# Joined streams in the split projections, and an earlier residual and first weights in the last layer, in a two-layer attention and state-space backbone

## The chip, the cores and the metric

One core of one Trainium2 chip. The metric is device time in microseconds (us) of one launch. Differences of 0.2% are about the smallest that a measurement of this kernel tells from none.

## What is computed

Two layers on two streams of 256 tokens with 1024 features: the latent stream x and the context stream ctx. Layer 0 mixes tokens by attention, layer 1 by a state-space scan; each mixer and each feed-forward part (1024 to 4096, squared relu, back to 1024) ends in a residual, a gate and a layer norm. Only the latent stream leaves the last layer.

```python
h_lat = layer_norm(ALPHA * h_lat + g_m_l * y_lat, ln_mix_g[i], ln_mix_b[i])
f_lat = squared_relu_mlp(modulate(h_lat, sh_f_l, sc_f_l), ff_w1[i], ff_w2[i])
h_lat = layer_norm(ALPHA * h_lat + g_f_l * f_lat, ln_ff_g[i], ln_ff_b[i])
```

In layer 0 the context stream takes the same three lines with its own modulation. All is float32.

## The kernel before, in words

**Products.** Activations lie features by tokens: eight tiles of 128 features, each 512 columns wide, columns 0 to 255 latent (stream 0) and 256 to 511 context (stream 1). Each weight and each activation is split into a high part (rounded to the format fp32r) and a low part, and a product is three matmuls: high by high, high by low, low by high. `gemm` (L83) runs eight k steps of these three for one output tile of 128 features, with the weights stationary and 256 or 512 columns of activations moving. In the last layer `down` (L278) turns this round: 128 tokens stationary, 512 weight columns moving.

**Weights.** `emit_w` (L46) loads two units with one transfer of 1 MB into one of two raw buffers, on the SyncE queue, and splits each: a cast to the high part on ScalarE (L61), a subtraction for the low part on VectorE (L62), in two halves. The pairs lie in a ring of four (`wsp`); `next_w` (L64) prepares the pair it returns and two ahead. A cast into the ring waits until TensorE has finished with the pair that lay there.

**Split order in layer 0.** `proj` (L346) multiplies the eight output tiles once for each stream, 256 columns at a time, with the context stream three tiles (`LAG`) behind the latent one, so that the latent layer norm can start while context tiles run. After tiles 3 and 7 of a stream, `colsum` (L212) adds the residual's columns up for the mean. It is used for the attention output (name ao) and for the last chunk (c = 3) of the feed-forward part down (name f0b); the first chunk up (name f0a, c = 0) in `ff` (L404) has the same lag, so that latent hidden tiles cover the context norm. All other tiles of layer 0 run 512 columns at once (`proj_joint`, L366). `ln` (L260) normalises a stream and splits it; its names are lm00 and lm01 after the attention, lf00 and lf01 after the feed-forward part, the last digit being the stream. `mods_sums` (L139) builds the modulation vectors of layer 1 on VectorE (tiles ma) from transfers into tiles wm; it is woven into `ff`, but runs ahead of its place where VectorE is free.

**Last layer.** The scan runs in four groups; while the last one (`ssd`, tiles y) runs, the output projection's first 12 of 16 k steps are woven in (`so`, L1059). Then (L1068 to L1083) the residual is transposed from features by tokens to tokens by features into Xt (L1079 to L1081, tiles xr), and for each tile of 128 tokens the last four k steps run for each half of 512 features, `add_half` (L290) adds the gated product and takes statistics, and `ln_mid` (L311) normalises, transposes (tiles ut) and splits into u4h and u4l. Then (L1087 to L1097) the first 512 hidden features of each token tile are multiplied (f1r), squared and turned by `hidden_rows` (L388), four pairs of weights being taken from the ring. The other hidden tiles are f1a, the products down f. The rows for the last norm (`row`, L272) are loaded at L1099, and the residual is scaled and shifted by them in chunk 1 (L1121).

**Order.** The program is written as one sequence; a scheduler of the framework then plans, from its own cost estimates, in which order each engine issues, by place in the program where several are ready. Attention (and some groups marked in the code) keep the written order. Each engine and each queue then runs strictly in its planned order.

Of the kernel before, what the change touches and what calls it, by code (L numbers as in the profile page):

```python
# [8 lines left out]
F32 = mybir.dt.float32  # L9
# [10 lines left out]
LAG = 3  # L20
# [19 lines left out]
class Net:  # L40
# [270 lines left out]
    def ln_mid(self, i, x, st, aff, uh, ul):  # L311
# [5 lines left out]
        for q in range(2):  # L317
# [4 lines left out]
            for m in range(4):  # L322
# [3 lines left out]
                nc.scalar.activation(uh[k][:, c], p, AF.Identity, bias=sh, scale=sc)  # L326
# [5 lines left out]
                nc.vector.tensor_sub(ul[k][:, c], t, uh[k][:, c].bitcast(F32))  # L332
# [13 lines left out]
    def proj(self, nm, ah, al, g, streams, lag, sums):  # L346
        nc = self.nc
        ws = {}
        for t in range(8 + lag):
            for s in streams[::-1]:  # L350
                m = t - (lag if s == 1 else 0)
                if not 0 <= m < 8:
                    continue
                if m not in ws:
                    ws[m] = self.next_w()
                ps = self.bank("mm", f"{nm}{s}{m}")[:, :256]
                self.gemm(ps, ws[m], ah, al, 256 * s, 256 * s + 256)
                x = self.X[s][:, m, :]
                nc.vector.scalar_tensor_tensor(x, ps, g[:, s, m:m + 1], x, op0=ALU.mult, op1=ALU.add)
# [4 lines left out]
                yield s, m  # L364

    def proj_joint(self, nm, ah, al, g):  # L366
        nc = self.nc
        for m in range(8):
            w = self.next_w()
            ps = self.bank("mm", f"{nm}{m}")  # L370
            self.gemm(ps, w, ah, al, 0, 512)
            for s in range(2):
                x = self.X[s][:, m, :]
                nc.vector.scalar_tensor_tensor(x, ps[:, 256 * s:256 * s + 256], g[:, s, m:m + 1], x,  # L374
                                               op0=ALU.mult, op1=ALU.add)
            yield m
# [11 lines left out]
    def hidden_rows(self, i, ps, fs):  # L388
# [4 lines left out]
        nc.vector.tensor_mul(r, r, r)  # L393
        pt = self.bank("aux", f"rt{i}")
# [9 lines left out]
    def ff(self, nm, uh, ul, g, streams, sums, mid=None):  # L404
        for c in range(4):
# [12 lines left out]

            if c == 0:
                for t in range(8 + LAG):  # L420
                    if t >= LAG:
                        hid(t - LAG, [1])
                    if t < 8:
                        hid(t, [0])
                    yield
            else:
                for m in range(8):
                    hid(m, streams)
                    yield
            fh = [fs[m][1] for m in range(8)]  # L430
            fl = [fs[m][2] for m in range(8)]
            if c < 3:
                for m in self.proj_joint(f"{nm}b{c}", fh, fl, g):
                    yield
            else:
                for s, m in self.proj(f"{nm}b{c}", fh, fl, g, streams, LAG, sums if c == 3 else None):
                    if c == 3 and m == 7 and mid is not None:
                        mid(s)
                    yield
# [275 lines left out]
    def layer0(self):  # L715
# [39 lines left out]
        with tc.tile_pool(name="wm", bufs=2) as self.wm:  # L755
# [8 lines left out]
            with tc.tile_pool(name="t2", bufs=4) as self.t2:  # L764
# [4 lines left out]
                for s, m in self.proj("ao", oh, ol, mT[:, :, 16:24], (0, 1), LAG, sums):  # L769
# [115 lines left out]
    def ssm_in(self, g, uh, ul):  # L885
# [19 lines left out]
        xw = [sp.tile([128, 2, 512], F32, tag=f"xw{d}", name=f"xw{g}{d}") for d in range(2)]  # L905
# [125 lines left out]
    def layer1(self):  # L1031
# [11 lines left out]
        nc.scalar.activation(self.aneg, self.vec("alog"), AF.Exp)  # L1043
        with tc.tile_pool(name="dq", bufs=1, space=DRAM) as dqp:
            dq = dqp.tile([2, 64, 256], F32, name="dq")
            self.dq = dq
            with tc.tile_pool(name="sp", bufs=2) as sp:
                self.sp = _Multi(tc, sp, dict(cy=2, ct=1, B=1, C=2, xt0=2, xt1=2, xw0=1, xw1=1, Bt=1, xc=1,
# [9 lines left out]

                def so():  # L1059
# [7 lines left out]
        with tc.tile_pool(name="tk", bufs=1) as self.tk, tc.tile_pool(name="fp1", bufs=2) as fp:  # L1067
            X = self.tk.tile([128, 2, 1024], F32, name="Xt")  # L1068
            ws = [self.next_w(whole=True, ahead=0) for _ in range(4)]
            bn = [self.stat_tile(f"bm{i}") for i in range(2)]  # L1070
            for i in range(2):
                for h in range(2):
                    for k in range(12, 16):
                        self.down(acc, st(yh, k), st(yl, k), ws[k - 12], k, k == 15, (i,), (h,))
                    if h == 0:
                        for q in range(2):
                            pt = self.bank("aux", f"xr{i}{q}")
                            for m in range(4):
                                nc.tensor.transpose(pt[:, 128 * m:128 * m + 128],  # L1079
                                                    self.X[0][:, 4 * q + m, 128 * i:128 * i + 128], self.ident)  # L1080
                            nc.scalar.copy(X[:, i, 512 * q:512 * q + 512], pt)  # L1081
                    self.add_half(acc, i, h, self.gates[2], X[:, i, :], bn[i])
# [146 lines left out]
```

## Time and profile before

| what | value |
|---|---|
| median of 3 runs | 1158.67 us (1158.28 to 1159.89) |
| profiled execution, its time | 1158.66 us |
| profiled execution, span of its instructions | 1156.9 us |
| TensorE matmuls, busy | 1098.6 us, 95% of the span, 6976 instructions |
| weight loads of TensorE, busy | 905.6 us, 78% |
| VectorE busy | 836.0 us, 72% |
| ScalarE busy | 603.3 us, 52% |
| GpSimd busy | 47.4 us, 4% |
| read from memory | 180.41 MB, 157 GB/s over the span |

PE is TensorE, PEld its weight loads, DVE VectorE, ACT ScalarE, SP SyncE. Matmuls overlap in the records, since one starts before the one ahead has left the engine, so the time that one costs is read from start to start. The granted clock is a share of full speed; 1.00 is 2.4 GHz and 0.50 is 1.2 GHz.

### The profile page before, as it was taken

Reading aid. Unit: us, or ns where it says so; the run is one execution under the profiler, and the core shown is the slowest. Engines: PE = TensorE matmul, PEld = TensorE weight load, DVE = VectorE, ACT = ScalarE, POOL = GpSimd, SP = SyncE. Lnnn points to the kernel's source line nnn. Section 1 sums busy time; section 2 is a strip of 40 time slices with the busy share of each in tenths; the row PEclk is TensorE's granted clock in tenths of the full one; section 3 lists DMA queues with packets and bytes.
Section 4 is the critical chain, followed back from the end, with each engine's and each line's share of the span. In section 5 each row is a group of like instructions: output and inputs, shape, how many; then the busy total and the mean of one; then the engine's idle time right before and its main releaser. Section 6 shows DMA issues by size and latency. Waiting matters only on the chain.

```text
span 1156.9 us, 18520 instructions
## 1 busy us (share of the span) xinstructions
PE 1098.6 (95%) x6976; PEld 905.6 (78%) x6976; DVE 836.0 (72%) x1701; ACT 603.3 (52%) x1382; POOL 47.4 (4%) x79
## 2 busy tenths in 40 slices
PE   5989999998999999999999998999999996999996
PEld 4776776988988887878899876777777675898895
DVE  4499885769938667773434899989799778565566
ACT  4386776135412322421423747787879756454451
POOL 1200000004000000000000410000000000000000
PEclk9999999999999999999999999999999998999999
DMA  8833442532635466663223135444445653555552
GB/s 318 330 128 115 124 131 90 182 111 74 201 127 184 164 221 232 231 205 108 74 74 110 46 114 155 156 146 145 147 139 189 224 199 142 172 182 193 182 182 73
DMA packets 41433, 182.79 MB, mean 158 GB/s; under 512 B 4608, under 2 KB 5248, under 8 KB 28288
## 3 DMA queue, kind: packets, MB, share of 16 engines
q1 hardware_dynamic: 41056, 181.36, 46.5%
q8 instruction: 55, 0.90, 0.3%
q10 hardware_dynamic: 288, 0.26, 0.1%
q14 instruction: 34, 0.28, 0.1%
HBM read 180.41 MB, written 1.18 MB: 157 GB/s over the span
## 4 chain that ended last, share of the span: by engine, by line
PE 80%; DVE 9%; DMA 5%; ACT 4%; issue 1%; DVEq 0%; SPq 0%; ACTq 0%
PE f0a L87 5%; PE f0a L88 5%; PE f0b L87 5%; PE f0a L89 5%; PE f0b L88 5%; PE f0b L89 5%; PE y L998 3%; PE f L288 2%; PE f L287 2%; PE f L286 2%; PE f1a L89 2%; PE f1a L87 2%; PE f1a L88 2%; DMA wm<-in_w_mod 2%; PE q L78 2%; PE pt L79 2%
## 5 line engine op out<-in xcount | busy, mean ns | idle before, releaser
L61 ACT CAST wh<-raw 128x512 fp32r<-128x512 f32 x404 | 238.6, 621 | 368.1 <-PE f0b L88 127.4
L62 DVE TENSOR_TENSOR wl<-raw,wh 128x512 fp32r<-128x512 f32 x404 | 269.0, 688 | 109.8 <-ACT wh L61 109.1
L87 PE MATMUL f0b<-f0fh,wh 128*128 128x512 f32 (+1 forms) x320 | 113.6, 355 | 0.0
L87 PE MATMUL f0a<-u1h,wh 128*128 128x512 f32 (+1 forms) x320 | 111.4, 352 | 1.5 <-ACT u1h L193 1.5
L88 PE MATMUL f0b<-f0fl,wh 128*128 128x512 f32 (+1 forms) x320 | 111.6, 349 | 0.1
L88 PE MATMUL f0a<-u1l,wh 128*128 128x512 f32 (+1 forms) x320 | 111.5, 350 | 0.0
L89 PE MATMUL f0b<-f0fh,wl 128*128 128x512 f32 (+1 forms) x320 | 111.2, 348 | 0.0
L89 PE MATMUL f0a<-u1h,wl 128*128 128x512 f32 (+1 forms) x320 | 111.2, 349 | 0.0
L150 DVE SCALAR_TENSOR_TENSOR ma<-wm,cs,ma 128x1024 f32<-128x1024 f32 x70 | 89.0, 1283 | 23.9 <-DMA wm<-in_w_mod 23.8
L87 PEld LDWEIGHTS f0a<-u1h,wh 128*128 128x128 f32 x320 | 60.9, 192 | 10.7 <-ACT u1h L193 2.1
L87 PEld LDWEIGHTS f0b<-f0fh,wh 128*128 128x128 f32 x320 | 60.1, 188 | 10.5 <-issue 2.6
L88 PEld LDWEIGHTS f0b<-f0fl,wh 128*128 128x128 f32 x320 | 60.1, 188 | 9.9 <-issue 1.4
L88 PEld LDWEIGHTS f0a<-u1l,wh 128*128 128x128 f32 x320 | 61.1, 192 | 8.2 <-DVE ut L195 0.4
L89 PEld LDWEIGHTS f0a<-u1h,wl 128*128 128x128 f32 x320 | 61.1, 191 | 7.6
L89 PEld LDWEIGHTS f0b<-f0fh,wl 128*128 128x128 f32 x320 | 60.2, 188 | 8.3
L87 PE MATMUL f1a<-u4h,wh 128*128 128x256 f32 x224 | 63.5, 284 | 0.0
L89 PE MATMUL f1a<-u4h,wl 128*128 128x256 f32 x224 | 63.5, 283 | 0.0
L88 PE MATMUL f1a<-u4l,wh 128*128 128x256 f32 x224 | 63.5, 283 | 0.0
L981 ACT ACTIVATE W<-A,sT 128x128 f32<-128x128 f32 (+1 forms) x128 | 50.0, 458 | 5.7 <-PE y L998 5.1
L374 DVE SCALAR_TENSOR_TENSOR X<-f0b,mT,X 128x256 f32<-128x256 f32 x48 | 21.0, 479 | 43.9 <-PE f0b L89 43.9
L89 PE MATMUL x<-u2h,wl 128*128 128x512 f32 x128 | 51.3, 402 | 1.1 <-DVE wl L62 1.1
L88 PE MATMUL x<-u2l,wh 128*128 128x512 f32 x128 | 51.6, 403 | 0.0
(435 smaller groups left out, 2702.7 us busy)
## 6 DMA issues: line engine op xcount, KB each, us to landing
raw<-in_wall SPq DMA_DIRECT2D x102, 1024.0 KB, 5.0
wm<-in_w_mod SPq DMA_DIRECT2D x96, 512.0 KB, 4.5
A<-dq SPq DMA_DIRECT2D x32, 256.0 KB, 3.6
E<-dq SPq DMA_DIRECT2D x32, 256.0 KB, 3.4
X<-in_xT SPq DMA_DIRECT2D x8, 256.0 KB, 7.4
gate<-in_rows SPq DMA_DIRECT2D x2, 512.0 KB, 12.3
out_dram<-Xt SPq DMA_DIRECT2D x4, 256.0 KB, 2.0
mixg<-in_rows SPq DMA_DIRECT2D x1, 512.0 KB, 6.2
```

Source lines behind the costliest of these rows:

```text
L61: nc.scalar.copy(h, src[:, c])
L62: nc.vector.tensor_sub(l, src[:, c], h.bitcast(F32))
L78: self.mm = lambda *a, **k: self.tc.keep_in_program_order(self.nc.tensor.matmul(*a, **k))
L79: self.tr = lambda *a, **k: self.tc.keep_in_program_order(self.nc.tensor.transpose(*a, **k))
L87: mm(ps, wh[:, k, :], ah[k][:, c0:c1], start=(k == 0), stop=False)
L88: mm(ps, wh[:, k, :], al[k][:, c0:c1], start=False, stop=False)
L89: mm(ps, wl[:, k, :], ah[k][:, c0:c1], start=False, stop=(k == 7))
L150: nc.vector.scalar_tensor_tensor(t, wm, c, t, op0=ALU.mult, op1=ALU.add)
L286: mm(ps, lh(i), wh[:, c], start=(k == 0), stop=False)
L287: mm(ps, ll(i), wh[:, c], start=False, stop=False)
L981: nc.scalar.activation(W[:, h, o:o + l1 - l0], A[:, h, l0:l1], AF.Relu, scale=-1.0, bias=self.sT[:, st, r + h:r + h + 1])
L998: ins = mm(ps[64 * a:64 * a + 64, l0:l1], lh[:, hc:hc + 64], mv, start=(n == 0), stop=(n == 5))
```

## The change

`proj` and `proj_joint` become one function: without split, eight joint tiles; with split, four joint tiles, then tiles 4 to 7 of the latent stream, then those of the context stream. In `ff` the first chunk up runs four latent tiles, the same four for the context, then four joint ones. `LAG` is 4 instead of 3. In the last layer, the residual's transposes go into the woven loop `so`, into tiles that the scan has left (their pool now outlives the scan); the first three weight pairs of the hidden part go into tiles of their own (those in which the rows for the last norm will lie), and the fourth pair is prepared behind tile 0's last split; tile 0's first hidden rows are multiplied ahead of tile 1's norm; the squared rows are turned after hidden tiles 4 and 5; the rows for the last norm are loaded in chunk 1.

```diff
-LAG = 3
+LAG = 4
...
-        t = self.tk.tile([128, 1024], F32, tag="row", name=nm, bufs=4)
+        t = self.tk.tile([128, 1024], F32, tag="row", name=nm, bufs=6)
...
+    def res_rows(self, x, i, q):
+        nc = self.nc
+        pt = self.bank("aux", f"xr{i}{q}")
+        for m in range(4):
+            nc.tensor.transpose(pt[:, 128 * m:128 * m + 128], self.X[0][:, 4 * q + m, 128 * i:128 * i + 128], self.ident)
+        nc.scalar.copy(x[:, 512 * q:512 * q + 512], pt)
...
-    def proj(self, nm, ah, al, g, streams, lag, sums):
+    def proj(self, nm, ah, al, g, split=False, sums=None):
+        cut = 8 - LAG if split else 8
...
+        for m, ss in [(m, (0, 1)) for m in range(cut)] + [(m, (s,)) for s in range(2) for m in range(cut, 8)]:
+            if m not in ws:
+                ws[m] = self.next_w()
+            n = 256 * len(ss)
+            ps = self.bank("mm", f"{nm}{ss[0]}{m}")[:, :n]
+            self.gemm(ps, ws[m], ah, al, 256 * ss[0], 256 * ss[0] + n)
+            for i, s in enumerate(ss):
                 x = self.X[s][:, m, :]
-                nc.vector.scalar_tensor_tensor(x, ps, g[:, s, m:m + 1], x, op0=ALU.mult, op1=ALU.add)
+                nc.vector.scalar_tensor_tensor(x, ps[:, 256 * i:256 * i + 256], g[:, s, m:m + 1], x,
+                                               op0=ALU.mult, op1=ALU.add)
                 if sums is not None and m % 4 == 3:
...
+            order = [(m, streams) for m in range(8)]
             if c == 0:
-                for t in range(8 + LAG):
-                    if t >= LAG:
-                        hid(t - LAG, [1])
-                    if t < 8:
-                        hid(t, [0])
-                    yield
...
+                order = [(m, (s,)) for s in streams for m in range(LAG)] + order[LAG:]
+            for m, ss in order:
+                hid(m, ss)
+                yield
...
                     for k in range(12):
                         self.down(acc, st(yh, k), st(yl, k), self.next_w(whole=True), k, False)
+                        if k % 2 and k > 3:
+                            i, q = divmod((k - 5) // 2, 2)
+                            if q == 0:
+                                X.append(self.xwp.tile([128, 1024], F32, tag=f"xw{i}", name=f"Xt{i}"))
+                            self.res_rows(X[i], i, q)
                         yield
...
+            first_w = []
+            for n in range(3):
+                wh, wl = (self.tk.tile([128, 1024], F32R, tag="row", name=f"f1w{n}{p}", bufs=6) for p in "hl")
+                self.emit_w(self.wpos, [(wh[:, 512 * q:512 * q + 512], wl[:, 512 * q:512 * q + 512]) for q in range(2)])
...
+            def f1_rows(i):
+                ps = self.bank("aux", f"f1r{i}")
...
+                return self.rows_sq(i, ps)
...
             for i in range(2):
                 for h in range(2):
                     for k in range(12, 16):
                         self.down(acc, st(yh, k), st(yl, k), ws[k - 12], k, k == 15, (i,), (h,))
...
+                    self.add_half(acc, i, h, self.gates[2], X[i], bn[i])
+                if i:
+                    with tc.issue_after(turned[0].ins), tc.issue_after(turned[1].ins):
+                        first_w.append(self.next_w(whole=True, ahead=0))
+                    rows.append(f1_rows(0))
+                turned = self.ln_mid(i, X[i], bn[i], aff, u4h, u4l)
+            rows.append(f1_rows(1))
...
+                    if c == 0 and m < 6:
+                        self.rows_turn(m - 4, rows[m - 4], first)
...
                 if c == 1:
+                    ag, ab = self.row(2, "mixg1"), self.row(3, "mixb1")
+                    fg, fb = self.row(4, "ffg1"), self.row(5, "ffb1")
```

`ln_mid` now returns its last ScalarE and its last VectorE instruction of the splits (`turned`), and `hidden_rows` is cut in two: `rows_sq` (relu and square) and `rows_turn` (transposes and splits).

## Rows read from the trace of the kernel before

**Rows 1.** The chain of waits over the span, shares by engine (page part 4).

```profile
PE 80%; DVE 9%; DMA 5%; ACT 4%; issue 1%; DVEq 0%; SPq 0%; ACTq 0%
```

**Rows 2.** Stretches: length, busy us (instructions) by engine, granted clock, DMA share, GB/s.

```profile
237.80:241.10 3.30, 3.30 (x18) 3.30 (x17) 0.20 (x1) 0.00 (x0) 0.00 (x0) 0.50 0.89 333
275.40:278.60 3.20, 3.15 (x15) 3.15 (x15) 3.20 (x9) 1.47 (x3) 2.81 (x4) 0.50 0.02 5
279.00:315.00 36.00, 36.00 (x301) 35.95 (x300) 35.42 (x64) 19.00 (x44) 4.97 (x5) 1.00 0.51 162
...
953.00:960.30 7.30, 0.03 (x1) 0.00 (x0) 7.24 (x20) 5.81 (x15) 0.00 (x0) 0.84 0.41 145
...
991.00:1142.00 151.00, 151.00 (x935) 136.27 (x935) 87.43 (x159) 74.61 (x156) 0.00 (x0) 1.00 0.51 175
```

**Rows 3.** Waits of TensorE, 204 to 320 and 930 to 992: us, times, longest.

```profile
PE aosum L208 <- DVE X L359: 2.0, 2, 1.8
PE f0a L87 <- ACT u1h L193: 1.5, 1, 1.5
PE lm01wb L241 <- DVE lm01wd L240: 1.2, 1, 1.2
PE lm01wt L232 <- ACT lm01ws L229: 0.5, 1, 0.5
...
PE ut L321 <- DVE Xt L315: 7.3, 1, 7.3
PE rt L396 <- DVE rr L393: 3.2, 2, 1.8
```

**Rows 4.** Instructions by tile: count, ns (minimum/median/maximum), first and last start; f0a, f0b.

```profile
L89 PE MATMUL f0a<-u1h,wl x78: 281/283/284, 284.8 to 312.7; 128*128 128x256 f32 x78
...
L89 PE MATMUL f0b<-f0fh,wl x30: 279/279/280, 590.7 to 601.0; 128*128 128x256 f32 x30
...
L89 PE MATMUL f0b<-f0fh,wl x28: 397/398/398, 315.8 to 334.7; 128*128 128x512 f32 x28
...
L87 PE MATMUL f0a<-u1h,wh x25: 389/389/390, 569.6 to 585.9; 128*128 128x512 f32 x25
...
L87 PEld LDWEIGHTS f0a<-u1h,wh x320: 186/188/333, 257.6 to 585.7; 128*128 128x128 f32 x160
```

**Rows 5.** Timeline of VectorE in the output projection: start, us, instruction [idle time before].

```profile
230.74 1.28 DVE L150 SCALAR_TENSOR_TENSOR ma<-wm,cs,ma 128x1024 f32<-128x1024 f32 x1 [1.96 <-DMA wm<-in_w_mod]
...
263.65 0.47 DVE L359 SCALAR_TENSOR_TENSOR X<-ao,mT,X 128x256 f32<-128x256 f32 x1
```

**Rows 6.** Timeline of ScalarE before the latent norm; in brackets the idle time before.

```profile
241.43 1.14 ACT L61 CAST wh<-raw 128x512 fp32r<-128x512 f32 x2 [8.75 <-PE ao L88]
245.74 0.37 ACT L220 COPY lm00ms<-aosum 128x256 f32<-128x256 f32 x1 [3.17 <-PE aosum L208]
```

**Rows 7.** Timeline of TensorE in the last layer, between projection and hidden tiles.

```profile
941.67 1.04 PE L1079 MATMUL xr<-con,X 128*128 128x128 f32 x8
...
949.92 1.06 PE L321 MATMUL ut<-con,Xt 128*128 128x128 f32 x8
...
960.36 1.94 PE L321 MATMUL ut<-con,Xt 128*128 128x128 f32 x8 [7.33 <-DVE Xt L315]
961.95 0.77 PE L1094 MATMUL f1r<-wh,u4h 128*128 128x512 f32 x1
...
978.75 0.37 PE L87 MATMUL f1a<-u4h,wh 128*128 128x256 f32 x1
```

**Rows 8.** Groups of VectorE instructions, 942 to 960 and 960 to 970: busy us, mean ns.

```profile
L62 DVE TENSOR_TENSOR wl<-raw,wh 128x512 fp32r<-128x512 f32 x6 | 3.9, 675 | 0.0
...
L1121 DVE TENSOR_TENSOR Xt<-Xt,mixg 128x512 f32<-128x512 f32 x4 | 2.7, 685 | 0.0
```

**Rows 9.** DMA issues by line: KB each, us from issue to landing.

```profile
ffb<-in_rows SPq DMA_DIRECT2D x1, 512.0 KB, 8.6
```

**Rows 10.** Instructions on tiles ma, 279 to 315: count, ns, first and last start.

```profile
L150 DVE SCALAR_TENSOR_TENSOR ma<-wm,cs,ma x12: 1272/1277/1496, 283.0 to 312.4; 128x1024 f32<-128x1024 f32 x12
```

More of the change, by code (lines that the diff above doesn't have):

```diff
@@ L331, in ln_mid @@
                     nc.vector.tensor_scalar(t, p, sc, sh, op0=ALU.mult, op1=ALU.add)
-                nc.vector.tensor_sub(ul[k][:, c], t, uh[k][:, c].bitcast(F32))
+                v = nc.vector.tensor_sub(ul[k][:, c], t, uh[k][:, c].bitcast(F32))
+        return a, v
     def ln_out(self, i, x, st, g, b):
@@ L363, in proj @@
                     self.colsum(sums[s], [(n, self.X[s][:, n, :]) for n in range(m - 3, m + 1)])
[L364 to L376, printed above, removed]
+            yield ss[-1], m
     def hidden(self, ps, c0, c1, fh, fl):
@@ L393, in hidden_rows, with rows_turn @@
         nc.vector.tensor_mul(r, r, r)
+        return r
+    def rows_turn(self, i, r, fs):
+        nc = self.nc
         pt = self.bank("aux", f"rt{i}")
@@ L417, in hid @@
                 self.hidden(ps, c0, c1, fh, fl)
+            order = [(m, streams) for m in range(8)]
             if c == 0:
-                for t in range(8 + LAG):
-                    if t >= LAG:
-                        hid(t - LAG, [1])
-                    if t < 8:
-                        hid(t, [0])
-                    yield
[L426 to L429, printed above, removed]
+                order = [(m, (s,)) for s in streams for m in range(LAG)] + order[LAG:]
+            for m, ss in order:
+                hid(m, ss)
+                yield
             fh = [fs[m][1] for m in range(8)]
             fl = [fs[m][2] for m in range(8)]
[L432 to L439, printed above, removed]
+            for s, m in self.proj(f"{nm}b{c}", fh, fl, g, c == 3, sums if c == 3 else None):
+                if c == 3 and m == 7 and mid is not None:
+                    mid(s)
+                yield
     def rope(self, dst, src):
@@ L768, in layer0 @@
                 nc.scalar.activation(warm[:, 0:1], self.eps, AF.Sqrt)
-                for s, m in self.proj("ao", oh, ol, mT[:, :, 16:24], (0, 1), LAG, sums):
+                for s, m in self.proj("ao", oh, ol, mT[:, :, 16:24], True, sums):
                     if m == 7:
@@ L904, in ssm_in @@
         G["xt"] = [sp.tile([128, 2, 512], F32, tag=f"xt{d}", name=f"xt{g}{d}") for d in range(2)]
-        xw = [sp.tile([128, 2, 512], F32, tag=f"xw{d}", name=f"xw{g}{d}") for d in range(2)]
+        xw = [self.xwp.tile([128, 2, 512], F32, tag=f"xw{d}", name=f"xw{g}{d}") for d in range(2)]
         Bt = sp.tile([128, 2, 128], F32, tag="Bt", name=f"Bt{g}")
@@ L1043, in layer1 @@
         nc.scalar.activation(self.aneg, self.vec("alog"), AF.Exp)
+        self.xwp = self.ctx.enter_context(tc.tile_pool(name="xwp", bufs=1))
         with tc.tile_pool(name="dq", bufs=1, space=DRAM) as dqp:
@@ L1057, in layer1 @@
                 st = lambda y, k: (lambda i: y[k % 8][:, 256 * (k // 8) + 128 * i:256 * (k // 8) + 128 * i + 128])
+                X = []
                 def so():
@@ L1067, in layer1 @@
         with tc.tile_pool(name="tk", bufs=1) as self.tk, tc.tile_pool(name="fp1", bufs=2) as fp:
-            X = self.tk.tile([128, 2, 1024], F32, name="Xt")
             ws = [self.next_w(whole=True, ahead=0) for _ in range(4)]
+            first_w = []
+            for n in range(3):
+                wh, wl = (self.tk.tile([128, 1024], F32R, tag="row", name=f"f1w{n}{p}", bufs=6) for p in "hl")
+                self.emit_w(self.wpos, [(wh[:, 512 * q:512 * q + 512], wl[:, 512 * q:512 * q + 512]) for q in range(2)])
+                self.wpos += 1
+                self.wout += 1
+                first_w.append((wh, wl))
+            self.fp = _Multi(tc, fp, dict(fh=9, fl=9, r=2, q=2))
+            pair = lambda m: tuple(self.fp.tile([128, 256], F32R, tag=t, name=f"f1{t}{m}") for t in ("fh", "fl"))
+            first = [pair(m) for m in range(4)]
+            def f1_rows(i):
+                ps = self.bank("aux", f"f1r{i}")
+                c = slice(128 * i, 128 * i + 128)
+                for k in range(8):
+                    wh, wl = (w[:, 512 * (k % 2):512 * (k % 2) + 512] for w in first_w[k // 2])
+                    nc.tensor.matmul(ps, u4h[k][:, c], wh, start=(k == 0), stop=False)
+                    nc.tensor.matmul(ps, u4l[k][:, c], wh, start=False, stop=False)
+                    nc.tensor.matmul(ps, u4h[k][:, c], wl, start=False, stop=(k == 7))
+                return self.rows_sq(i, ps)
             bn = [self.stat_tile(f"bm{i}") for i in range(2)]
+            rows = []
             for i in range(2):
@@ L1127, in layer1 @@
                         self.down(acc, lh(m), ll(m), ws[m - 4], 24 + m, m == 7, (i,), (h,))
[L1128 to L1129 removed]
+                    self.add_half(acc, i, h, self.gates[5], X[i], bn[i])
+                self.ln_out(i, X[i], bn[i], fg, fb)
     def chain(self, *gs):
```

43 lines of the change are left out of this document (4 added, 39 removed).

## The prediction

> **What bounds the kernel now.** I read the chain of waits first, because it says which engine's work the end hangs on: TensorE carries 80% of it [rows 1]. So only two things shorten the run: fewer TensorE microseconds, or fewer gaps in them. The table by stretches shows where the gaps are [rows 2]: in 279 to 315 us TensorE is busy for all 36 us, in 953.0 to 960.3 for 0.03 of 7.3. The waits of TensorE name them [rows 3]. In layer 0 it waits 2.0 us for column sums of the attention output, then 0.5, 1.2 and 1.5 us in the layer norm of the context stream; in the last layer 7.3 us for the normalised rows of the second token tile and 3.2 us for the squared rows. Two of the gaps are paid twice: after them the granted clock is 0.50, the lower of its two levels, 237.8 to 241.1 and 275.4 to 278.6 [rows 2].
>
> **A. Joined tiles.** Four of eight output tiles at each of three places (attention output, first feed-forward chunk up, last chunk down) become one 512-column product instead of two of 256. One tile is 8 x 3 products, so 96 pairs a place. Start to start, from first and last start over count [rows 4]: 256 columns take (312.7 - 284.8)/(3 x 77) = 0.1208 us where the modulation sums still run, 0.1184 in the last chunk; 512 columns take (334.7 - 315.8)/(3 x 27) = 0.2333 just after the first, (585.9 - 569.6)/(3 x 24) = 0.2264 before the second. Two places give 96 x (0.2416 - 0.2333) = 0.8 each, the third 96 x (0.2368 - 0.2264) = 1.0: **2.6 us**. Ends: 1.9 with 0.2333 at the third place too, 3.9 with 0.2264 everywhere; I keep each place with the stretch it is nearest to. VectorE still adds each stream by itself, so nothing is saved there.
>
> Joining also halves the weight loads of those tiles. One shows 0.188 us [rows 4], but a product starts every 0.1208, so the loads run beside the products, and I count nothing for them.
> The Trainium skill, TensorE: Matmul & The Clock Gate, Part 3 under "The mechanism", says that a weight load overlaps a product in flight only when the row groups differ; these loads and products all use the full 128 rows. By that rule the 288 loads saved would add 288 x 0.188 = 54 us. The trace does not agree with it.
>
> A joined first tile needs the context columns of the last head pair, which the half tile did not, but only in the last of its eight k steps, and seven (21 x 0.2333 = 4.9 us) stand before that. I count 0; without that cover it is at most the half tile that now runs beside the end of attention, 24 x 0.1208 = 2.9.
>
> **B. Context norm.** The order becomes joint 0 to 3, latent 4 to 7, context 4 to 7, then latent hidden 0 to 3 before context hidden. The norm of the context stream is now covered by four latent hidden tiles instead of three: 24 x 0.1208 = 2.9 us against the 3.2 us that TensorE waits there. Its start does not come later: the last context add stood on VectorE until 263.65 [rows 5], behind the splits of the latent stream, and these start from the last latent tile as before. With the gap nearly gone I also give back the half clock: 3.2 us hold 15 products that take 1.8 at 0.1208, so 1.4. **4.3 us**; ends 0 (VectorE decides, below) and 4.6.
>
> **C. Column sums.** 1.8 of the 2.0 us is one wait at 236.6. VectorE was late because a modulation sum ahead of the add had waited 1.96 us for its transfer [rows 5]; half clock follows, 1.4 again. Now the sums come behind joint tile 3, with four latent tiles that need none of it. But the modulation sums stay on the same queue, and whether one is late depends on a transfer. Ends 0 and 3.2; no row is nearer to either, I take the middle, **1.6 us**.
>
> Weights in the split tiles: four prepared pairs are live there, and the next cast on ScalarE waits until a context tile has let go of its pair, as it does now (idle 8.75 us before the cast at 241.43 [rows 6]). The pairs for tiles 4 to 7 become free while joint tiles of 5.6 us run, so TensorE does not see it. Cost 0; the loss if it is queued badly is a rival.
>
> **D. Last layer.** Reference is 941.67, where the first quarter of the last products ends, to 978.75, where the hidden tiles start: 37.1 us [rows 7].
> - Products: 36 x 0.2264 = 8.2. The transposes of tile 0 now are ready under them: second half at 2.7, then the 4.5 us of add, statistics and normalising that the trace shows (941.67 + 1.0 of residual transposes + 2.7 = 945.4, to 949.92), so 7.2. Transposes 1.1, up to 0.5 for the first split: 9.8.
> - First hidden rows of tile 0, 24 x 0.2264 = 5.4, now run while tile 1 is added and normalised. The fourth weight pair is cast only after tile 0's last split (queued on ScalarE and VectorE), and k steps 6 and 7 are behind it on TensorE, and tile 1's transposes behind those: a cast and a subtraction of 0.6 to 0.7 us each, some 1.2 us late. 16.4.
> - Tile 1: from transposes to first product 961.95 - 960.36 = 1.6; rows 5.4: 23.4. Both waits for squared rows fall, since hidden tiles 4 and 5 run meanwhile; the turns themselves stay, 1.3: 24.7.
> - The residual's 16 transposes (1.04 for eight) are paid in the y group instead: 2.1. Each also takes one of three auxiliary banks and a ScalarE copy there; the next y sums wait for them at most a copy's 0.6.
> - The first three pairs have places of their own, so their six subtractions on VectorE come before the normalising of tile 0 and no longer after the products. I charge three of six, 3 x 0.6 = 1.8 (six took 3.9 [rows 8]), since they are due before the adds in program order.
> 37.1 - 24.7 - 2.1 - 1.8 = **8.5 us**. Helping: VectorE spends 2.7 us on four instructions with one row for the last norm in the critical stretch [rows 8], and as much on four with the other. These eight and their two scalings on ScalarE now come in chunk 1, at no cost: VectorE is busy 87 of 151 us there, ScalarE 75 [rows 2]; without that cover it is their 5.4 us. Ends: 3.1 if tile 0's rows do not cover tile 1 (8.5 - 5.4), 10.3 if the subtractions cost nothing.
>
> The four row transfers leave the y group for the hidden stage. There the DMA engines are 0.51 busy (991 to 1142 [rows 2]); I count 0. If they all go ahead of a weight load, it lands as late as the fourth row did, 8.6 us after issue [rows 9], against 5.6 us for two pairs: 3 us.
>
> **Sum.** 2.6 + 4.3 + 1.6 + 8.5 = 17.0. The profiled execution took 1158.66 (span 1156.9), the median of the runs is 1158.67, so no correction: **1141.7 us**. All low ends give 5.0 us, all high ends 22.0.
>
> **Rivals.**
> 1. VectorE decides in layer 0. For: it is busy 35.42 of 36 us in 279 to 315 [rows 2]. Against: twelve of its instructions there, 1.28 us each, are modulation sums [rows 10] that nothing waits for yet. Then A's first two places, B and C come to nothing: 1.0 + 8.5 = 9.5, 1149.2 us.
> 2. The order planned for the last layer runs tile 1's work ahead of tile 0's rows, or the fourth pair comes so late that they cover nothing. For: the late fourth pair. D loses 5.4: 1147.1 us.
> 3. Slower. ScalarE runs in order. In the two places where a norm follows, the casts of the four next pairs wait for the four context tiles, and if they stand ahead of the copy of the latent sums, the latent norm starts up to 4 x 24 x 0.1208 = 11.6 us late instead of 0.7. Price 10.9 + 1.4 of clock, twice, 24.6: 1158.7 - 17.0 + 24.6 = 1166.3 us. It decides from the third cast: 8.0 + 1.4, twice, is 18.8. For: a cast that waited 8.75 us stood directly ahead of the copy at 245.74 [rows 6]. Against: that cast was done 3 us before the copy could run.
> 4. The change moves its waits and removes none: the context norm comes as much later as its cover grows, and tile 1's rows come as late as now because the first pairs' subtractions push them back. For: VectorE is shared by all of these. Against: they are 3.6 us, not 17. Then only A counts, half of it given back: 1157.4 us.
> 5. Weight loads stand in the way of products and joining removes them: 17.0 - 2.6 + 54 = 68, 1090 us. Against: 0.1208 is less than one load.
> The Trainium skill page named above is the source of this one; its rule is what the 0.1208 us speak against.
>
> **How the numbers follow.** Forecast 0.55, rivals 0.17, 0.16, 0.07, 0.04 and 0.01. A measurement of this kernel tells about 0.2% (2.3 us) from no change. Faster: 0.55 + 0.17 + 0.16 + 0.01 = 0.89; same 0.04; slower 0.07. The range runs from 1135 (just beyond the high ends) to 1152 (rival 1, with the 3 us of the row transfers): it holds the forecast with rivals 1 and 2, 0.88, less a little for their tails.
>
> **What would show it.** Right: 512-column products at 0.227 to 0.233 us for four tiles at three places; no wait of TensorE above 1 us around the context norm and no granted clock of 0.5 there; the 7.3 us wait replaced by one of 1 to 2 us; no wait for squared rows. Wrong: hidden tiles at more than 0.121 us a product (rival 1); a wait of several us ahead of tile 0's rows, or of their sixth k step (rival 2); a cast that idles ScalarE ahead of the copy of the sums (rival 3); the y group more than 2 us longer (rival 4).

## The result, and the profile after

| | before | after |
|---|---|---|
| median (lowest to highest), us | 1158.47 (1156.68 to 1159.89) | 1147.36 (1145.92 to 1150.04) |
| ratio, 95% interval | | 0.9915 (0.9898 to 0.9932) |
| profiled execution: time, span, us | 1158.66, 1156.9 | 1150.04, 1148.2 |
| TensorE matmuls, busy us, instructions | 1098.6, 6976 | 1095.5, 6688 |
| VectorE, ScalarE busy, us | 836.0, 603.3 | 834.3, 600.1 |

The change makes the kernel 11.1 us faster by the medians, 9.8 by the ratio (0.0085 x 1158.47), where 17.0 was forecast. The profiled execution of after is 2.7 us above its median.

The shares of the chain of waits, the answer to [rows 1]: TensorE's fell from 80% to 75%, so waits for others weigh more than before.

```profile
PE 75%; DVE 10%; DMA 8%; ACT 5%; issue 2%; DVEq 0%; SPq 0%; ACTq 0%
```

TensorE's waits of after (us, times, longest), in the stretches of [rows 3] and, first, in 640 to 720 us, where the scan stage begins:

```profile
PE B L87 <- DVE z L875: 3.4, 1, 3.4
PE x L87 <- DVE cy L800: 1.6, 1, 1.6
...
PE aosum L208 <- DVE X L368: 2.7, 2, 1.5
PE f0a L87 <- ACT u1h L193: 0.3, 1, 0.3
...
PE ut L329 <- DVE Xt L323: 3.0, 1, 3.0
PE f1r L1088 <- ACT rr L390: 0.8, 1, 0.8
PE f1a L87 <- ACT r L380: 0.7, 1, 0.7
...
```

The context norm's 3.2 us have shrunk to 0.3. In the last layer the 7.3 us for the normalised rows of tile 1 (the second token tile) and the 3.2 for the squared rows are gone; in their place TensorE waits 3.0 us for the rows of tile 0. The column sums' wait has not shrunk (2.7 against 2.0). New is the first line: B, a product of the scan stage, waits 3.4 us until VectorE has done z.

The same by stretches (length, busy us by engine, granted clock), the answer to [rows 2]:

```profile
237.80:241.10 3.30, 2.12 (x18) 1.43 (x18) 1.46 (x2) 0.37 (x1) 0.00 (x0) 1.00 0.34 78
...
272.00:306.00 34.00, 34.00 (x195) 29.57 (x195) 33.00 (x59) 16.79 (x36) 8.36 (x8) 1.00 0.45 155
...
649.80:654.00 4.20, 0.68 (x2) 0.19 (x2) 4.20 (x12) 2.17 (x5) 3.28 (x5) 0.81 0.00 0
654.00:657.20 3.20, 3.18 (x8) 2.50 (x9) 3.07 (x6) 0.77 (x2) 2.48 (x2) 0.50 0.11 18
...
948.20:951.20 3.00, 0.04 (x1) 0.08 (x2) 3.00 (x8) 0.29 (x1) 0.00 (x0) 1.00 0.00 0
952.80:956.20 3.40, 3.13 (x8) 2.48 (x8) 2.76 (x10) 2.62 (x8) 0.00 (x0) 0.50 0.00 0
```

The clock is full in both old places of half clock (row one, and 272 to 306 behind the context norm). It is 0.50 in two others, each shortly behind an idle TensorE: 0.68 us busy of 4.2 ahead of 654.0, 0.04 of 3.0 ahead of 951.2 (a third, at 707 us, is in the last section). The second is not new in kind: in the kernel before, the clock was 0.50 behind the wait of 7.3 us too, in this row of before:

```profile
960.30:964.60 4.30, 4.24 (x14) 3.74 (x15) 4.30 (x11) 2.06 (x6) 0.00 (x0) 0.50 0.44 124
```

VectorE is as full beside the hidden tiles as before (33.0 of 34), and TensorE does not wait there.

Where the time came from, in first starts of tiles on TensorE (us from the span's start):

| | before | after | gained so far |
|---|---|---|---|
| f0a, first chunk up | 257.6 | 254.1 | 3.5 |
| f0b, first chunk down | 314.6 | 306.1 | 8.5 |
| z, first product of the scan stage | 638.2 | 627.3 | 10.9 |
| x, behind dt, B and C | 676.4 | 670.0 | 6.4 |
| so, the output projection | 887.7 | 883.6 | 4.1 |
| last product f | 1147.2 | 1138.5 | 8.7 |

Up to z the gain is 10.9 us. Some 2 us of it are chance: in the run of the last layer alone (below), whose layer 0 is that of before, z starts at 636.2, and against that the gain is 8.9, near the 8.5 forecast for layer 0. Between z and x, within some 40 us, 4.5 were lost. The other stages differ between executions of one kernel: in a second profile of the changed kernel (below, "unedited again") z to x loses 3.6, x to so gains 1.1 where it loses 2.3 here, and so to the last f gains 2.1 where it gains 4.6 here.

### The profile page after: what moved, and what is told of

The parts are those of the page before. It is cut to its first block, busy times and chain, and to the rows that moved or that the text cites. A ratio compares the mean times of both kernels' runs of the same rounds, so it can differ in the third digit from the quotient of the medians.

```text
span 1148.2 us, 17915 instructions
## 1 busy us (share of the span) xinstructions
PE 1095.5 (95%) x6688; PEld 888.5 (77%) x6688; DVE 834.3 (73%) x1693; ACT 600.1 (52%) x1374; POOL 48.7 (4%) x79
## 4 chain that ended last, share of the span: by engine, by line
PE 75%; DVE 10%; DMA 8%; ACT 5%; issue 2%; DVEq 0%; SPq 0%; ACTq 0%
PE f0a L87 5%; PE f0b L87 5%; PE f0a L88 5%; PE f0a L89 5%; PE f0b L89 5%; PE f0b L88 5%; PE y L991 3%; PE f L288 2%; PE f L287 2%; DMA raw<-in_wall 2%; PE f L286 2%; DMA wm<-in_w_mod 2%; PE f1a L87 2%; DMA E<-dq 2%; PE f1a L89 2%; PE f1a L88 2%
## 5 line engine op out<-in xcount | busy, mean ns | idle before, releaser
L62 DVE TENSOR_TENSOR wl<-raw,wh 128x512 fp32r<-128x512 f32 x398 | 264.2, 686 | 102.6 <-ACT wh L61 102.1
L87 PE MATMUL f0a<-u1h,wh 128*128 128x512 f32 (+1 forms) x288 | 105.3, 369 | 0.3 <-ACT u1h L193 0.3
L88 PE MATMUL f0b<-f0fl,wh 128*128 128x512 f32 (+1 forms) x288 | 105.5, 366 | 0.0
L88 PE MATMUL f0a<-u1l,wh 128*128 128x512 f32 (+1 forms) x288 | 105.4, 368 | 0.0
L89 PE MATMUL f0a<-u1h,wl 128*128 128x512 f32 (+1 forms) x288 | 105.1, 366 | 0.0
L368 DVE SCALAR_TENSOR_TENSOR X<-f0b,mT,X 128x256 f32<-128x256 f32 x64 | 28.2, 478 | 58.5 <-PE f0b L89 58.5
L87 PEld LDWEIGHTS f0a<-u1h,wh 128*128 128x128 f32 x288 | 53.8, 188 | 11.7 <-ACT u1h L193 1.0
L87 PEld LDWEIGHTS f0b<-f0fh,wh 128*128 128x128 f32 x288 | 54.1, 188 | 11.1 <-issue 2.2
L89 PEld LDWEIGHTS f0b<-f0fh,wl 128*128 128x128 f32 x288 | 54.1, 188 | 9.6
L89 PEld LDWEIGHTS f0a<-u1h,wl 128*128 128x128 f32 x288 | 54.3, 189 | 9.2 <-issue 0.4
L88 PEld LDWEIGHTS f0a<-u1l,wh 128*128 128x128 f32 x288 | 54.2, 189 | 8.9 <-DVE ut L195 0.4
L87 PE MATMUL x<-u2h,wh 128*128 128x512 f32 x128 | 51.0, 398 | 1.6 <-DVE cy L800 1.6
```

Source lines behind the costliest of these rows:

```text
L62: nc.vector.tensor_sub(l, src[:, c], h.bitcast(F32))
L87: mm(ps, wh[:, k, :], ah[k][:, c0:c1], start=(k == 0), stop=False)
L88: mm(ps, wh[:, k, :], al[k][:, c0:c1], start=False, stop=False)
L89: mm(ps, wl[:, k, :], ah[k][:, c0:c1], start=False, stop=(k == 7))
L368: nc.vector.scalar_tensor_tensor(x, ps[:, 256 * i:256 * i + 256], g[:, s, m:m + 1], x, op0=ALU.mult, op1=ALU.add)
```

## The experiments

Us gained are (1 - ratio) x the median of the kernel before in the same rounds. "z to x" is the first start of x less that of z, in the profiled execution; before 38.2, after 42.7. The rows are three groups of four, each run beside the kernel before; between groups only the ratios compare.

| run | ratio (95% interval) | gained, us | z to x, us |
|---|---|---|---|
| layer 0 alone | 0.9962 (0.9948 to 0.9975) | 4.4 | 42.5 |
| last layer alone | 0.9942 (0.9928 to 0.9955) | 6.7 | 38.1 |
| dt's accumulator moved | 0.9924 (0.9909 to 0.9938) | 8.8 | 37.4 |
| subtractions late | 0.9911 (0.9897 to 0.9925) | 10.3 | 42.7 |
| unedited again | 0.9913 (0.9889 to 0.9936) | 10.1 | 41.8 |
| last chunk in old order | 0.9884 (0.9860 to 0.9907) | 13.4 | 39.5 |
| dt moved and subtractions late | 0.9886 (0.9863 to 0.9908) | 13.2 | 37.5 |
| old order and subtractions late | 0.9876 (0.9853 to 0.9899) | 14.4 | 39.8 |
| layer 0 alone, last chunk in old order | 0.9919 (0.9894 to 0.9944) | 9.4 | 38.2 |
| three split tiles | 0.9899 (0.9873 to 0.9926) | 11.7 | 38.4 |
| residual back | 0.9906 (0.9880 to 0.9932) | 10.9 | 43.0 |
| old order, dt moved, subtractions late | 0.9886 (0.9859 to 0.9914) | 13.2 | 36.3 |

**The two halves.** The kernel before with only layer 0's part of the change (first diff, and the changed `ff`), and the changed kernel with `proj`, `proj_joint` and `ff` of before (second diff):

```diff
-LAG = 3
+LAG = 4
...
-        for t in range(8 + lag):
-            for s in streams[::-1]:
...
+        for m, ss in [(m, (0, 1)) for m in range(cut)] + [(m, (s,)) for s in range(2) for m in range(cut, 8)]:
```

```diff
-LAG = 4
+LAG = 3
...
-        for m, ss in [(m, (0, 1)) for m in range(cut)] + [(m, (s,)) for s in range(2) for m in range(cut, 8)]:
...
+        for t in range(8 + lag):
+            for s in streams[::-1]:
```

> Only the split projections of layer 0 and their order (parts A to C), with the last layer as before. Theory G (layer 0 gains about 10.4 us up to the dt product, and some 6 of them are given back at the start of the scan stage, where VectorE has the splits of the context norm to do before it empties the banks of z): 4 to 5 us in all, 1153.5 to 1154.5 us, with a wait of TensorE for z of about 3.4 us ahead of B and half clock behind it. Rival H (nothing is given back for good; the profiled run of the changed kernel merely shows a stall of its own, and the parts are worth what the prediction said): 8.5 us or more, 1150 us or less, and no such wait. If the give-back is larger still, up to 1157.

> Only the last layer's new order, the residual turned in the y group and the places of the first three pairs (part D), with layer 0 as before. Theory S (VectorE does the six subtractions of the pairs ahead of tile 0's adds, so D is worth 4.5 to 5 us and not 8.5): 1153.5 to 1154.5 us, with a wait of about 3 us for tile 0's normalised rows. Rival (D is worth its 8.5 us and the loss belongs to layer 0 alone): 1150 us. Together with the run of layer 0 alone, if the parts add up: the two gains sum to 11.1 us.

They gave 4.4 us (2.9 to 6.0) and 6.7 (5.2 to 8.3), together 11.1, so the parts add up. Layer 0 is what theory G said, with the wait of 3.4 us for z; the forecast's 8.5 is outside its interval. The last layer lies between its theories: more than 4.5 to 5, and 8.5 is just outside its interval.

**What gives layer 0's gain back.** Why B waits shows in VectorE's timeline (start, us, instruction). One z is the end of one of six z tiles; it frees the accumulator that TensorE needs next. lf01wb marks the start of the context norm's splits. The kernel before:

```profile
655.05 0.42 DVE L882 SCALAR_TENSOR_TENSOR z<-con,z 128x256 f32<-128x256 f32 x1
658.75 1.29 DVE L265 TENSOR_TENSOR X<-X,lf01wb 128x512 f32<-128x512 f32 x2 [0.94 <-PE lf01wb L241]
662.92 1.27 DVE L265 TENSOR_TENSOR X<-X,lf01wb 128x512 f32<-128x512 f32 x2
666.83 0.41 DVE L882 SCALAR_TENSOR_TENSOR z<-con,z 128x256 f32<-128x256 f32 x1
667.77 0.42 DVE L882 SCALAR_TENSOR_TENSOR z<-con,z 128x256 f32<-128x256 f32 x1
```

The kernel after:

```profile
640.77 0.42 DVE L875 SCALAR_TENSOR_TENSOR z<-con,z 128x256 f32<-128x256 f32 x1 [0.55 <-ACT con L874]
645.48 1.28 DVE L265 TENSOR_TENSOR X<-X,lf01wb 128x512 f32<-128x512 f32 x2 [1.07 <-PE lf01wb L241]
649.65 1.27 DVE L265 TENSOR_TENSOR X<-X,lf01wb 128x512 f32<-128x512 f32 x2
653.56 0.41 DVE L875 SCALAR_TENSOR_TENSOR z<-con,z 128x256 f32<-128x256 f32 x1
654.50 0.42 DVE L875 SCALAR_TENSOR_TENSOR z<-con,z 128x256 f32<-128x256 f32 x1
656.06 0.41 DVE L875 SCALAR_TENSOR_TENSOR z<-con,z 128x256 f32<-128x256 f32 x1
```

Before, four z are done when the splits begin and two stand behind them. After, three and three. Four accumulators carry the tag that z, dt and B take in turn (the tag mm of the code): with three unread z and dt none is left, and B starts at 654.02, 0.05 us after the first late z ends. Two edits attack this, one by one. dt was given an accumulator of another tag:

```diff
...
-        ps = self.bank("mm", "dt")[:64, :]
+        ps = self.bank("md", "dt")[:64, :]
...
```

> The changed kernel, with the product dt moved to an accumulator of another tag, so that the z tiles and B share four banks among fewer takers. Theory K (what is given back at the start of the scan stage is a wait for a bank: B cannot start because VectorE has not emptied the z banks): the wait of 3.4 us and the half clock of 6.8 us behind it (another 3.4 us) shrink or fall, 2 to 6 us faster than the changed kernel, 1141 to 1145 us. Rival V (VectorE itself is late by the context norm's splits, and the bank only shows it): the wait turns up one product later, at x or at the next weights, and the time is within 1 us of the changed kernel, 1146.5 to 1148 us.

The wait for z ahead of B and the half clock behind it fell, and x started 5.3 us sooner after z. But the next waits in 640 to 720 us grew:

```profile
PE x L87 <- DVE cy L800: 2.0, 1, 2.0
PE x L89 <- DVE wl L62: 1.2, 1, 1.2
PE C L87 <- DVE z L875: 0.9, 1, 0.9
```

From x to the output projection this execution takes 215.0 us (after 213.6, unedited again 210.2, before 211.3), and the time is that of the unedited kernel within the intervals. So theory K falls as a price, and what rival V said, that the wait only moves, fits. It is not a clean test of the accumulator, because the scheduler planned the last layer anew as well: four of the six early subtractions (see The last layer) stand ahead of tile 0's first add there, and from that add to the last f it takes 195.0 us, where after takes 198.4.

The second edit leaves the accumulators alone and puts the third place (last chunk of the feed-forward part down) back into the order of before, in the changed kernel and in layer 0 alone:

```diff
...
+        if split and sums is not None and nm != "ao":
+            order = [(t - 3 * s, (s,)) for t in range(11) for s in (1, 0) if 0 <= t - 3 * s < 8]
...
```

> The changed kernel, but the last chunk's down projection of layer 0 (the third of the three places) in the order of the kernel before: eight tiles of each stream by itself, the context three tiles behind. Theory G (the third place gains 1 us of products and brings z so close behind the two norms that VectorE gives back 4 to 6 us at the start of the scan stage): from the first z product to the first x product 38 us as before and not 42.7, no wait for z ahead of B and no half clock at 652; the time is 2 to 4 us under that of the unedited changed kernel beside it. Rival V (VectorE's work from the context norm to the first y products decides, whatever order TensorE has): x starts earlier, but the first y products do not, and the time is within 1 us of the changed kernel, or 1 us over it for the products given up.

> Layer 0's part alone, as in the first run of the study, but without its third place: the last chunk's down projection in the order of the kernel before. Theory G (the third place is what gives the gain back, at the start of the scan stage): parts A's first two places, B and C are kept, 0.8 + 0.8 + 4.3 + 1.6 = 7.5 us, 1151 us on a kernel before of 1158.5, ratio 0.9935. Rival V (VectorE takes back what layer 0 gains, whatever order the third place has): 3 to 4.5 us, ratio 0.996 to 0.9975, as with the third place.

In layer 0 alone the gain rises from 4.4 to 9.4 us: 0.0043 in the ratio, with half-widths of 0.0014 and 0.0025, together 0.0029 (root of the sum of squares). Theory G had said 7.5, inside the 6.5 to 12.3 us of its interval. In the changed kernel it rises from 10.1 to 13.4 in the same rounds; 0.0029 there is within 0.0033. TensorE's waits of layer 0 alone with the old order, 560 to 730 us:

```profile
PE dt L87 <- ACT wdth L809: 1.9, 1, 1.9
PE xt L900 <- DVE X L795: 1.2, 1, 1.2
PE x L89 <- DVE wl L62: 1.0, 1, 1.0
```

Nothing waits for z ahead of B; z to x is 38.2 us, as before. So theory G holds in layer 0 alone: the third place gave back what the others had earned. In the changed kernel it is not shown so clearly. The wait for z is gone there too, but the half clock near 652 us, which theory G said would go, is still there in part (this row is of that run):

```profile
653.00:656.50 3.50, 3.33 (x10) 2.61 (x11) 3.50 (x10) 1.99 (x5) 2.59 (x4) 0.69 0.00 0
```

Here z to x is 39.5 and not 38, z itself starts 2.2 us later than in the unedited execution beside it (629.2 against 627.0), and x starts at the same time (668.7 against 668.8). That execution took 1147.34, against a median of 1144.89. The times lean to theory G without deciding it.

**Three split tiles.**

```diff
-LAG = 4
+LAG = 3
```

> The changed kernel with three split tiles a place instead of four: joint 0 to 4, latent 5 to 7, context 5 to 7, three latent hidden tiles ahead of context hidden. Theory B (the fourth tile covers the context norm): a wait of TensorE of 2.5 to 3.2 us comes back between latent hidden and context hidden, perhaps with half clock (1.7 us), against 0.3 us of products saved by the further joined tile at each place; at the third place z comes a little later, which by theory G gives back less: ratio to before 0.992 to 0.995, 1 to 4 us over the changed kernel. Rival (three tiles cover it as well, since the column sums come earlier): within 1 us of the changed kernel, 0.991.

The time, 0.9899, is nearer to the rival's 0.991 than to theory B's 0.992 to 0.995. Yet theory B is right where it speaks of waits: around the context norm TensorE waits as in [rows 3], and the clock drops behind it (waits in 200 to 320 us, then the stretch, of this run):

```profile
PE f0a L87 <- ACT u1h L193: 1.5, 1, 1.5
PE lm01wb L241 <- DVE lm01wd L240: 1.2, 1, 1.2
PE lm01wt L232 <- ACT lm01ws L229: 0.5, 1, 0.5
```

```profile
271.80:275.20 3.40, 3.27 (x15) 3.21 (x16) 3.40 (x9) 1.55 (x4) 2.93 (x4) 0.52 0.03 5
```

From the first f0a to the first f0b this run takes 55.4 us, after 52.0. What this costs comes back at the other end, where four z are done ahead of the splits again and z to x is 38.4:

```profile
651.51 0.42 DVE L875 SCALAR_TENSOR_TENSOR z<-con,z 128x256 f32<-128x256 f32 x1
655.21 1.28 DVE L265 TENSOR_TENSOR X<-X,lf01wb 128x512 f32<-128x512 f32 x2 [0.94 <-PE lf01wb L241]
659.38 1.27 DVE L265 TENSOR_TENSOR X<-X,lf01wb 128x512 f32<-128x512 f32 x2
663.29 0.41 DVE L875 SCALAR_TENSOR_TENSOR z<-con,z 128x256 f32<-128x256 f32 x1
```

So by the traces the fourth split tile earns 3.4 us where it covers the first context norm and costs 4.3 at the third place. Four at the first place and three at the third were not tried together.

**The last layer.** VectorE's timeline of after while tile 0 is added and normalised (add: gt, Xt; subtractions of the pairs: L62; end: Xt from lm10mv):

```profile
940.07 0.69 DVE L303 TENSOR_TENSOR gt<-so,gate 128x512 f32<-128x512 f32 x1 [1.44 <-PE so L288]
940.68 1.28 DVE L62 TENSOR_TENSOR f1w0l<-raw,f1w0h 128x512 fp32r<-128x512 f32 x2
941.88 1.28 DVE L62 TENSOR_TENSOR f1w1l<-raw,f1w1h 128x512 fp32r<-128x512 f32 x2
943.09 0.68 DVE L304 TENSOR_TENSOR Xt<-Xt,gt 128x512 f32<-128x512 f32 x1
...
944.68 1.29 DVE L62 TENSOR_TENSOR f1w2l<-raw,f1w2h 128x512 fp32r<-128x512 f32 x2 [0.31 <-ACT f1w2h L61]
...
947.09 0.68 DVE L303 TENSOR_TENSOR gt<-so,gate 128x512 f32<-128x512 f32 x1
...
950.21 0.80 DVE L323 TENSOR_SCALAR Xt<-Xt,lm10mv 128x1024 f32<-128x1024 f32 x1
```

All six subtractions run inside tile 0's chain, and so do four instructions of tile 1 (at 947.09, 948.29, 949.00 and 949.62). The run writes the preparation of the three pairs (transfer, cast, subtraction) behind tile 0's normalising:

```diff
...
     turned = self.ln_mid(i, X[i], bn[i], aff, u4h, u4l)
+    if not i:
+        for n in range(3):
...
```

> The changed kernel, with the six subtractions of the first three pairs written in the program behind the normalising of tile 0 instead of ahead of both tiles' products. Theory S (they hold up tile 0's adds): tile 0 is normalised some 2 to 4 us earlier, the wait of 3.0 us for its rows shrinks to under 1 us and the half clock of 952.8 to 956.2 falls with it (1.7 us): 1142.5 to 1144.5 us. Rival F (the splits and the fourth pair set the end anyway, or the subtractions that now come later hold up the first hidden rows in their place): within 1 us of the changed kernel, 1146.5 to 1148.5 us.

Its timeline and wait:

```profile
940.00 0.69 DVE L303 TENSOR_TENSOR gt<-so,gate 128x512 f32<-128x512 f32 x1 [1.43 <-PE so L288]
940.61 0.68 DVE L62 TENSOR_TENSOR f1w0l<-raw,f1w0h 128x512 fp32r<-128x512 f32 x1
941.21 0.69 DVE L304 TENSOR_TENSOR Xt<-Xt,gt 128x512 f32<-128x512 f32 x1
...
947.94 0.81 DVE L323 TENSOR_SCALAR Xt<-Xt,lm10mv 128x1024 f32<-128x1024 f32 x1
```

```profile
PE ut L329 <- DVE Xt L323: 0.8, 1, 0.8
```

The subtractions still run inside the chain, one at a time between the adds, and one instruction of tile 1 stands ahead of the normalising instead of four; the 2.2 us below belong to both. Tile 0 is normalised 2.2 us sooner after its first add (947.94 - 940.00 = 7.9 against 950.21 - 940.07 = 10.1), and the half clock behind the wait is gone (granted clock 1.00 in 951 to 954). From the first add to the last f the run takes 196.8 us; the two profiles of the unedited kernel take 198.4 and 198.7, the three other runs with late subtractions 196.4 to 196.7. The timed runs cannot confirm 2 us: 0.9911 against 0.9915 and 0.9913. So theory S is right by the traces, at some 2 us; its 3 to 5 us were too many.

**The residual.**

```diff
...
-                            self.res_rows(X[i], i, q)
...
+                    if h == 0:
+                        X.append(self.xwp.tile([128, 1024], F32, tag=f"xw{i}", name=f"Xt{i}"))
+                        for q in range(2):
+                            self.res_rows(X[i], i, q)
```

> The changed kernel with the residual's 16 transposes and four copies back in the last layer, behind each token tile's first half, as in the kernel before. The prediction counted the move at nothing in sum (2.1 us off the last layer, 2.1 us onto the y group). By that: within 1 us of the changed kernel, 0.991. Rival 1 (the y group hides them, TensorE waits for VectorE there): 2 us slower, 0.993. Rival 2 (in the last layer they stand where TensorE waits 3 us for tile 0's rows, and fill that wait): 1 to 2 us faster, 0.990.

No difference (0.9906). From so to the first add it takes 53.8 us (before 54.2, after 56.5), so the move costs the y group 2.7 us by these two, where 2.1 were charged. The wait for tile 0's rows is shorter with the transposes ahead of it, but a transpose now waits for the copy (930 to 992 and around it):

```profile
PE xr L295 <- ACT Xt L296: 1.8, 1, 1.8
PE ut L329 <- DVE Xt L323: 1.6, 1, 1.6
```

**Again, and together.** The unedited kernel stood beside three combinations.

> The changed kernel once more, unedited, on the same chip and in the same rounds as the three runs beside it. Ratio to the kernel before 0.990 to 0.993, as first measured. If the half clock of the first profile at 652 to 659 and 707 to 714 us belongs to the kernel, it is there again; what comes and goes (the half clock near 14 us, the one near 953) is chance.

> The changed kernel with both edits of the first four runs: dt's accumulator of another tag and the six subtractions written behind tile 0. If the trace of each alone tells the truth (start of the scan stage some 2.4 us earlier up to the last quarter, last layer 2 us shorter): 3 to 4.5 us under the unedited changed kernel, ratio about 0.988. Rival (each only moves a wait, as the timed runs of each alone suggest): within 1 us, ratio 0.991 to 0.992.

> The last chunk in the order of before and the six subtractions written behind tile 0, together. If both theories hold (G 2 to 4 us, S 2 us): 4 to 6 us under the unedited changed kernel, ratio 0.986 to 0.988. If only S holds: 2 us or less, ratio 0.990.

> Last chunk in the order of before, dt's accumulator of another tag, the six subtractions behind tile 0. If the edits were independent: ratio 0.984 to 0.986, some 2 us under the best of the runs so far. If dt's bank and the last chunk's order remove the same wait (after the old order there is no wait for z ahead of B): no better than the two without the bank's move, 0.987 to 0.989.

The wait for z ahead of B was there again, 3.4 us, and so were two of the stretches of low clock: 0.53 in 653.7 to 656.9 and, against the guess of chance, this one behind the wait for tile 0's rows:

```profile
950.40:953.80 3.40, 3.13 (x9) 2.44 (x9) 2.76 (x10) 2.62 (x8) 0.00 (x0) 0.57 0.00 0
```

The half clock at 707 us and the one near 14 us were not (last section). Moving dt with the subtractions late gave 13.2 us, more than either alone (8.8 and 10.3), though over the late subtractions alone the 0.0025 are within the noise of 0.0027; the old order with the subtractions late 14.4, all three 13.2. The bank and the old order do not add, as expected where both remove one wait. Old order with subtractions late is the best measured, as the best of several perhaps partly by luck, 1144.10 us (1142.52 to 1146.80) where the kernel before has 1158.66 and the unedited changed one 1147.99. Over the latter it is 0.0037 ahead, a little more than the 0.0033 of both half-widths together. The other parts of the last layer's change (tile 0's hidden rows ahead of tile 1's norm, the later turning, the later rows for the last norm) were not run apart.

## Why the prediction was right and where it was not

The sign and the range held; the sum was too high by 17.0 - 11.1 = 5.9 us. Of this 8.5 - 4.4 = 4.1 lie in layer 0 and 8.5 - 6.7 = 1.8 in the last layer. That the range held says little of the mechanism: it was wide enough for rivals 1 and 2. And that 1147.36 is almost rival 2's 1147.1 is coincidence, since D did not lose the 5.4 us of rival 2.

- **A held.** From start to start a joint product takes (305.5 - 284.1)/(3 x 31) = 0.230 us in the first chunk up and (598.8 - 577.5)/(3 x 31) = 0.229 in the last chunk down, within the forecast 0.227 to 0.233:

```profile
L87 PE MATMUL f0a<-u1h,wh x32: 389/389/477, 284.1 to 305.5; 128*128 128x512 f32 x32
...
L87 PE MATMUL f0b<-f0fh,wh x32: 394/394/397, 577.5 to 598.8; 128*128 128x512 f32 x32
```

- **B held in its place.** From the first f0a to the first f0b the kernel gained 5.0 us (57.0 to 52.0), for which 4.3 + 0.8 were forecast (52.1 in the second profile), and the run with three tiles brought the waits and the half clock back.
- **C failed in its step.** The waits for the column sums stayed, 2.7 us. Only the half clock behind them is absent, and in the run of the last layer alone, whose layer 0 is that of before, it is absent too: the granted clock in 200 to 260 us is 1.00 there, 0.97 before. So of C's 1.6 us nothing is shown to belong to the change. The 1.4 us for that half clock was itself taken over from B: its row has 18 products in 3.3 us, which take 2.2 at 0.1208, so 1.1.
- **The step that failed most is a cost put at nothing: what the new order of the third place does to the stage behind it.** The sum has only A's gain of 1.0 us for that place. I asked what four context tiles cover, and not what comes behind them. "The norm of the context stream is now covered by four latent hidden tiles" is true of the first chunk up; behind the last chunk it is covered by z tiles, which VectorE must empty, and one fewer was empty when the splits began: TensorE waited 3.4 us ahead of B, and layer 0 alone kept 4.4 us with that order and 9.4 without it. VectorE's queue was in the forecast only as rival 1, for the hidden tiles, where it did not decide: the last context hidden tiles, 272.97 to 283.98, take 0.121 us a product, no more than forecast.
- **D was mis-sized.** From the first add to the last f the gain is 6.9 us (205.3 to 198.4), where 37.1 - 24.7 - 1.8 = 10.6 were forecast ahead of the residual's 2.1. "I charge three of six" was one term: all six ran inside tile 0's chain, 3.9 us for 1.8, with four instructions of tile 1 among them, and the run that put them otherwise shortened that chain by 2.2 us. The other is the half clock. The prediction said that two gaps are paid twice, both in layer 0, and passed over the third, behind the 7.3 us; in the changed kernel the wait of 3.0 us is paid twice as well (eight products in 3.4 us, which take 1.8 at 0.2264: 1.6). Together 4.6 us, where 1.8 were charged.
- **Rival 2's sign**, a wait of several us ahead of tile 0's rows, came with its 3.0 us, but not for rival 2's reason alone: TensorE does not wait for the fourth pair, the wait for tile 1's rows is gone, and only VectorE ran some of tile 1's work ahead. The waits for squared rows are gone, and moving the residual made no difference, both as forecast.
- **Rival 3** did not come: no cast idles ScalarE ahead of the copy of the sums. **Rival 4** came in part: in layer 0 a wait moved to the next stage, and in the last layer the first pairs' subtractions pushed rows back, but tile 0's and not tile 1's. More than A's part is left, so it falls as a price.
- **Rival 5** fell. The weight loads' records lost 17.1 us (905.6 to 888.5) and TensorE's busy time 3.1; 288 loads are gone, and layer 0 alone gained 4.4 us, not 54 and more. The Trainium skill, TensorE: Matmul & The Clock Gate, Part 3 under "The mechanism", says in its list of what overlaps that a load overlaps a product in flight only where the row groups differ; the runs do not agree with that line.

## What to carry to other kernels

When a step is made to cover a wait, follow the covered engine to the next stage: the work that the cover hid is still on its queue, and what stands behind it there (here the emptying of three accumulators) is the next wait. One order need not suit all places where it is used: try each place by itself. Rank an early preparation behind the chain that it is to serve, or it joins that chain. And where a gap was seen to be followed by half clock, look for the same behind every other gap, and behind those that the change leaves.

## What was not expected

Some of the half clock comes and goes between executions of one kernel. Over the same stretch of the changed kernel, first in the first profile and then in the unedited run:

```profile
707.00:713.80 6.80, 6.48 (x13) 3.85 (x14) 6.65 (x13) 2.85 (x11) 0.00 (x0) 0.50 0.11 16
```

```profile
707.00:713.80 6.80, 6.16 (x21) 3.47 (x23) 6.80 (x13) 3.66 (x12) 0.00 (x0) 1.00 0.21 41
```

Thirteen instructions of TensorE in 6.8 us in one, 21 in the other (some 3 us further on in the program by then), at about the same busy time. In the first 60 us the granted clock is 1.00 before and in the unedited run, 0.94 in the first profile of after, though the change touches nothing there. Six timed runs of the unedited kernel spread from 1146.14 to 1151.16 us. So one profile cannot rank kernels 3 us apart: z to x and the named waits repeat, the end of the span does not.
